# State-space mixer: chunk ends by full-width table loads, whole state tiles, and a reordered gated unit

## The chip, the cores and the metric

The kernel runs on 1 core of one Trainium2 chip. The metric is device time in microseconds (us) of one execution. A profile of one execution of the kernel before is at hand, and three timed runs of it.

## The reference, cut to what matters

Six layers run over 256 positions of 1024 channels. Each of the first four is a mixer and a gated feed-forward layer; the second of these has the state-space mixer (S5), and only that mixer is touched here. It works in 64 groups of 16 channels, each with 64 complex states, once forward and once backward over the sequence:

```python
u = hf.reshape(b, s, S5_GROUPS, S5_GROUP)            # 64 groups of 16 channels
y_fwd = _s5_direction(u, ..., False)                 # h[t] = lam_bar * h[t-1] + B_bar u[t];  y[t] = Re(C h[t])
y_bwd = _s5_direction(u, ..., True)
y = (y_fwd + y_bwd).reshape(b, s, d) + d_skip * hf
g = gelu(y)
val, gate = split(g @ w_glu, 2, axis=-1)             # the gated unit
return val * sigmoid(gate)
```

## The kernel before, in words

All matrices that are not small are multiplied as three products of split weights (`whi`, `wlo`) and split activations; a slab of weights of 128x1024 is loaded by SP's queue, split by ACT (L170) and DVE (L171), and gives 12 products of 512 columns (L307 to L309). Everything is issued in the order in which the Python code runs; a small scheduler `S` only delays pieces of code by a number of ticks, and a slab gives two ticks.

The mixer (`S5.mix`) cuts the 256 positions into 32 chunks of 8. `U` holds the input so that a column is one chunk of one group: for group (m, q) the tile `u_of(m, q)` is 128 rows (8 positions of 16 channels) by 32 chunks. Tables made earlier turn this into chunk states and back:

- **Chunk ends** (`chunk_ends`, L1703 to L1715; `place`, L1717 to L1727). For each of eight k, eight matmuls with the 32 columns of `u_of` stationary and 256 table columns (`wb`) moving, four of them side by side in column tiles of 32. The result has chunks on its partitions, so ACT copies it to `ends` (L1715), PE transposes it in four pieces (L840), and DVE and ACT put the two directions (partitions 0 to 63 forward, 64 to 127 backward) into `es` (L1724, L1726, L1727). `es[0]` takes k = 0 to 3, `es[1]` takes k = 4 to 7.
- **The scan** (`scan_ops`, L1750). For each `es`, 30 steps over the chunks of three DVE operations each (L1757, L1758, L1761), so 90 operations. The first `ISC` = 45 operations of `es[0]`'s scan run alone; after that each of them is followed by one of `es[1]`'s. What is left of `es[1]`'s scan runs alone.
- **States copied** (`states`, L1766). At chunks 11, 23 and 30 the steps done are copied by ACT from `es` to `H` (L1771, L1772), four copies for each stretch: real and imaginary parts lie in two tiles `H`, each for both scans.
- **Outputs of the mixer** (`part`, L1776). Within a chunk: `u_of` stationary and a table `local` moving, for all k, while the scan runs. From the state at the chunk's start: `H` stationary and a table `ct` moving, for k = 0 to 3 after the first scan, for k = 4 to 7 after the second. The sums are in four PSUM banks `ybank`; DVE transposes a bank (L1850), ACT does the gelu (L1846), and ACT and DVE split it (L453, L454).
- **The gated unit** (`in_proj`). Sixteen slabs (b, s): output block b of 512 columns, input channels 256s to 256s+255. Slabs with s of 0 or 1 need the outputs of k = 0 to 3 alone, those with s of 2 or 3 also those of k = 4 to 7. Four slabs with s of 0 or 1 come first. The function `rest` (the products for k = 4 to 7 and their outputs) is put into the order of PE after `OR` = 6 ticks, so behind 36 products.

The tables for k = 3 to 7, `local` and `ct` come from DRAM by SP's queue; tiles of 128x2048 share 13 buffers. `taps` (L1573) makes `local` in the feed-forward layer before the mixer, by small matmuls (L1579).

Of the kernel before, what the change touches and what calls it, by code (L numbers as in the profile page):

```python
# [17 lines left out]
P = 128  # L18
# [17 lines left out]
BB = 12  # L36
AR = 13
GD = 3
ISC = 45


DS = (0, 1, 2, 3, 4, 4, 5, 5)
# [5 lines left out]
IK = 3  # L48
OB = 0
OS = 2  # L50
OR = 6
QD = 7
AE = 4
ISM = 1000
# [154 lines left out]
def tile_two_blocks(ctx: ExitStack, tc: tile.TileContext, A, out, upto=None, taps=None):  # L209
# [37 lines left out]
            o += [(b, s) for s in range(4)]  # L247
        return o

    def add_in(ap, nblk, base=0):  # L250
        for b, s in order_in(nblk):
            W.add(ap[base + b, s])

    def add_out(ap, nk, order=None):
# [4 lines left out]
    for i in (range(6) if upto is None else upto):  # L259
        if i >= 4:  # L260
            i -= 4
            layers.append(("ffn1", i))
            add_in(A["ffn1_in"][i], 11)
            add_out(A["ffn1_out"][i], 22)
            layers.append(("mix", i))
            for b, s in order_in(12)[:8]:
                W.add(A["mix_in"][i, b, s])
            W.add(A["mix_small"][i])
            for b, s in order_in(12)[8:]:
                W.add(A["mix_in"][i, b, s])  # L270
            add_out(A["mix_out"][i], 16)
            layers.append(("ffn2", i))
            add_in(A["ffn2_in"][i], 11)
            add_out(A["ffn2_out"][i], 22)
            continue
        kind = i % 3
        if kind == 0:
            layers.append(("fourier", i))
            W.add(A["dft_d"])
            W.add(A["dft_t"])  # L280
            add_out(A["fnet_w_out"][i // 3], 8)
        elif kind == 2:
            layers.append(("attention", i))
            add_in(A["qkv"], 18)
            add_out(A["attn_o"], 8, ATTN_OUT)
        else:
            layers.append(("s5", i))
            add_in(A["s5_glu"], 4)
        layers.append(("ffn", i))
        add_in(A["ffn_in"][i], 11)  # L290
        add_out(A["ffn_out"][i], 22)
# [119 lines left out]
            if i % 2 == 1:  # L411
                S.tick()

    def in_proj(xn, nblk, evict, src=None, after_head=None, bank=lambda b: acc()):

        head = {}
        for b, s in order_in(nblk):
# [883 lines left out]
    class S5:  # L1301
# [267 lines left out]
        def taps(self, m, ct):  # L1569
# [102 lines left out]
        def mix(self, xn, nxt):  # L1672
# [28 lines left out]
                return U[:, q * 512 + m * 32:q * 512 + (m + 1) * 32]  # L1701

            es = [big(F32, "es") for _ in range(2)]  # L1703
            ends = {}
# [12 lines left out]
            def place(k):  # L1717

                e = ends.pop(k)
                ps = transposed([e[:, u * 256 + r * P:u * 256 + (r + 1) * P] for r in range(2) for u in range(2)])  # L1720
                src = ps.rearrange("p (r g c) -> p r g c", r=2, g=8)
                dst = es[k // 4].rearrange("p (c r g) -> p r g c", r=2, g=32)[:, :, k % 4 * 8:k % 4 * 8 + 8]
                if k < 4:
                    nc.vector.tensor_copy(dst[:64], src[:64])  # L1724
                else:
                    nc.scalar.activation(dst[:64], src[:64], AF.Copy)  # L1726
                nc.scalar.activation(dst[64:], src[64:, :, :, ::-1], AF.Copy)  # L1727
# [16 lines left out]
            H = [big(F32, "H") for _ in range(2)]  # L1744
            for r in range(2):
                h = H[r].rearrange("p (g c) -> p g c", g=64)
                nc.gpsimd.memset(h[:64, :, 0:1], 0.0)
                nc.gpsimd.memset(h[64:, :, 31:32], 0.0)

            def scan_ops(w):  # L1750

# [4 lines left out]
                for c in range(1, 31):  # L1756
                    yield lambda: nc.vector.tensor_tensor(t, a8, e[:, c - 1, None].to_broadcast([P, 2, 2, 32]), OP.mult)  # L1757
                    yield lambda: nc.vector.tensor_tensor(e[:, c], e[:, c], t[:, 0], OP.add)  # L1758

                    def last():  # L1760
                        nc.vector.tensor_tensor(e[:, c], e[:, c], swapped, OP.add)  # L1761
                        if c in (11, 23, 30):
                            states(w, c - 11 if c < 30 else 24, c + 1)
                    yield last

            def states(w, c0, c1):  # L1766
                src = es[w].rearrange("p (c r g) -> p r g c", r=2, g=32)
                gs = slice(32 * w, 32 * w + 32)
                for r in range(2):
                    h = H[r].rearrange("p (g c) -> p g c", g=64)  # L1770
                    nc.scalar.activation(h[:64, gs, c0 + 1:c1 + 1], src[:64, r, :, c0:c1], AF.Copy)  # L1771
                    nc.scalar.activation(h[64:, gs, 31 - c1:31 - c0], src[64:, r, :, c0:c1][:, :, ::-1], AF.Copy)  # L1772

            ybank = [acc() for _ in range(4)]

            def part(k, i, local=None):  # L1776
                for s in range(2):
                    m = 2 * k + s
                    for q in range(4):
                        o = ybank[k // 2][32 * q:32 * q + 32, k % 2 * 256:(k % 2 + 1) * 256].rearrange(  # L1780
                            "p (j s k) -> p j s k", j=8, s=2)[:, :, s]
                        g = 4 * m + q
                        if i == 0:
                            lhs, rhs = u_of(m, q), local[:, m % 4 * 512 + q * P:m % 4 * 512 + (q + 1) * P]
                        else:
                            lhs = H[i - 1][:, g * 32:(g + 1) * 32]
                            at = s * 1024 + q * 256 + (i - 1) * P
                            rhs = self.ct[k][:, at:at + P]
                        nc.tensor.matmul(o, lhs, rhs, start=i == 0 and s == 0 and k % 2 == 0, stop=i == 2,
                                         skip_group_check=True, tile_position=(0, 32 * q))  # L1790

            local = [self.load_local(i) for i in range(4)]
            for k in range(4):
                self.load_ct(k)
            for k in range(8):
                part(k, 0, local[k // 2])
            for k in range(4, 8):
                self.load_ct(k, local[k - 4])
            first, second = scan_ops(0), scan_ops(1)
# [3 lines left out]
                    next(second)()  # L1803
            oT = Chunks(8)
            for k in range(4):
                for i in (1, 2):
                    part(k, i)
# [7 lines left out]

            def rest():
                for k in range(4, 8):
                    for i in (1, 2):
                        part(k, i)
# [256 lines left out]
```

## Time and profile before

| | us |
|---|---|
| median of 3 runs | 2505.49 (2505.14 to 2505.72) |
| the profiled execution | 2506.46 |
| its span in the trace | 2504.7 |
| PE busy | 2437.3 (97%) |
| DVE busy | 1620.1 (65%) |
| ACT busy | 1330.6 (53%) |

A row of the trace gives the time from the start of the span, the time taken, the engine and the line. PE is TensorE's matmuls, PEld its loads of the stationary operand. "x16" is a number of records; a float32 matmul leaves two records, each with a load and a product. Granted clock is that of TensorE, as a share of full speed: 1.00 is 2.4 GHz and 0.50 is 1.2 GHz. The chain of work that ended last is followed back from the end: each piece in it was released by the one before it.

### The profile page before, as it was taken

The page shows a single profiled execution, that of the slowest core. Times are in us where ns is not written, and L with a number is a line of the kernel's source. Part 1 is how long each engine was busy: PE and PEld are TensorE (multiplying, and loading weights), DVE is VectorE, ACT ScalarE, POOL GpSimd, SP SyncE. Part 2 cuts the span into 40 slices and gives each one's busy share as a digit, 9 for nine tenths or more (in the row PEclk, how much of TensorE's full clock was granted, in tenths as well). Part 3 has the DMA queues.
Part 4 walks back from the last instruction along what each step waited for, and adds up shares of the span by engine and source line. Part 5 has one row for each costly group of instructions (what it writes and reads, how often), then busy time and mean ns, then how long its engine had stood idle before and what let it go on. Part 6 is the DMA issues. An engine that isn't in the chain of part 4 may idle for free.

```text
span 2504.7 us, 34769 instructions
## 1 busy us (share of the span) xinstructions
PE 2437.3 (97%) x13048; PEld 2008.2 (80%) x13048; DVE 1620.1 (65%) x2855; ACT 1330.6 (53%) x2029; POOL 101.7 (4%) x123
## 2 busy tenths in 40 slices
PE   7999869999999999999999999999999999999998
PEld 6777658888878788888888888888888888788886
DVE  7989866555776665565555557875555555876554
ACT  5444565444565554444444446765444445775543
POOL 0011000000043200000000000000000000000000
PEclk9999979999999999999999999999999999999999
DMA  5798655565555455535555554545556565535554
GB/s 173 235 285 250 239 206 187 183 200 189 164 164 175 146 185 184 188 125 190 191 180 190 192 181 153 178 135 188 181 185 195 176 188 176 193 121 168 185 185 143
DMA packets 132424, 460.53 MB, mean 184 GB/s; under 512 B 14857, under 2 KB 23956, under 8 KB 129312
## 3 DMA queue, kind: packets, MB, share of 16 engines
q1 hardware_dynamic: 124192, 431.16, 53.3%
q0 software_dynamic: 7488, 26.51, 3.3%
q8 instruction: 102, 1.67, 0.3%
q10 hardware_dynamic: 576, 0.66, 0.1%
q14 instruction: 66, 0.54, 0.1%
HBM read 441.76 MB, written 20.69 MB: 185 GB/s over the span
## 4 chain that ended last, share of the span: by engine, by line
PE 88%; DVE 7%; ACT 4%; issue 1%; DMA 0%; POOL 0%; ACTq 0%; DVEq 0%; POOLq 0%
PE acc L307 26%; PE acc L308 26%; PE acc L309 26%; DVE wlo L171 2%; PE aux L473 2%; PE aux L840 1%; DVE conv L1002 1%; ACT whi L170 1%; PE aux L381 1%; PE aux L745 1%; PE aux L696 1%; PE aux L722 1%; PE aux L1579 0%; PE aux L1238 0%; PE aux L659 0%
## 5 line engine op out<-in xcount | busy, mean ns | idle before, releaser
L171 DVE TENSOR_TENSOR wlo<-raw,whi 128x1024 fp32r<-128x1024 f32 (+1 forms) x774 | 924.6, 1218 | 386.9 <-ACT whi L170 380.7
L170 ACT ACTIVATE whi<-raw 128x1024 fp32r<-128x1024 f32 (+1 forms) x774 | 794.2, 1056 | 319.7 <-PE acc L309 294.6
L307 PE MATMUL acc<-whi,xhi 128*128 128x512 f32 (+1 forms) x2104 | 836.6, 398 | 2.4 <-DVE yflo L519 2.4
L308 PE MATMUL acc<-wlo,xhi 128*128 128x512 f32 (+1 forms) x2104 | 819.9, 390 | 7.4 <-DVE wlo L171 7.4
L309 PE MATMUL acc<-whi,xlo 128*128 128x512 f32 (+1 forms) x2104 | 819.7, 390 | 0.0
L308 PEld LDWEIGHTS acc<-wlo,xhi 128*128 128x128 f32 x2104 | 396.8, 189 | 85.8 <-DVE wlo L171 9.8
L307 PEld LDWEIGHTS acc<-whi,xhi 128*128 128x128 f32 x2104 | 396.8, 189 | 84.8 <-issue 4.4
L309 PEld LDWEIGHTS acc<-whi,xlo 128*128 128x128 f32 x2104 | 396.2, 188 | 82.7
L307 PE MATMUL acc<-whi,yhi 128*128 128x512 f32 x976 | 386.2, 396 | 2.4 <-ACT whi L170 0.9
L308 PE MATMUL acc<-wlo,yhi 128*128 128x512 f32 x976 | 380.8, 390 | 3.2 <-DVE wlo L171 3.2
L309 PE MATMUL acc<-whi,ylo 128*128 128x512 f32 x976 | 381.0, 390 | 0.0
L484 ACT ACTIVATE silu<-acc,rsq 128x256 f32<-128x256 f32 x176 | 83.6, 475 | 304.2 <-PE acc L309 304.2
L485 DVE SCALAR_TENSOR_TENSOR hb<-acc,rsq,silu 128x256 f32<-128x256 f32 x176 | 84.5, 483 | 222.6 <-ACT silu L484 222.5
L308 PEld LDWEIGHTS acc<-wlo,yhi 128*128 128x128 f32 x976 | 183.4, 188 | 41.2 <-DVE wlo L171 4.8
L307 PEld LDWEIGHTS acc<-whi,yhi 128*128 128x128 f32 x976 | 183.3, 188 | 41.0 <-ACT whi L170 1.3
L309 PEld LDWEIGHTS acc<-whi,ylo 128*128 128x128 f32 x976 | 183.2, 188 | 39.6 <-DVE ylo L454 0.9
L453 ACT ACTIVATE yhi<-aux 128x512 fp32r<-128x512 f32 (+1 forms) x104 | 54.3, 562 | 105.2 <-PE aux L473 102.7
L454 DVE TENSOR_TENSOR ylo<-aux,yhi 128x512 fp32r<-128x512 f32 (+1 forms) x104 | 63.7, 644 | 56.6 <-ACT yhi L453 56.5
L390 ACT ACTIVATE xhi<-aux,gains 128x256 fp32r<-128x256 f32 x104 | 40.7, 475 | 82.2 <-PE aux L381 82.2
L392 DVE SCALAR_TENSOR_TENSOR xlo<-aux,gains,xhi 128x256 fp32r<-128x256 f32 x104 | 43.1, 477 | 49.9 <-ACT xhi L390 49.9
L436 DVE SCALAR_TENSOR_TENSOR x<-acc,x 128x512 f32<-128x512 f32 x52 | 35.5, 690 | 55.9 <-PE acc L309 55.9
L715 POOL TENSOR_SCALAR sc<-sc,st 128x512 f32<-128x512 f32 x28 | 46.7, 1673 | 268.7 <-DVE st L713 256.9
(361 smaller groups left out, 1794.1 us busy)
## 6 DMA issues: line engine op xcount, KB each, us to landing
raw<-in_ffn_in_dram SPq DMA_DIRECT2D x352, 512.0 KB, 4.3
raw<-in_ffn_out_dram SPq DMA_DIRECT2D x176, 512.0 KB, 4.3
raw<-in_mix_in_dram SPq DMA_DIRECT2D x96, 512.0 KB, 3.6
raw<-in_qkv_dram SPq DMA_DIRECT2D x72, 512.0 KB, 4.1
raw<-in_mix_out_dram SPq DMA_DIRECT2D x32, 512.0 KB, 3.7
raw<-in_fnet_w_out_dram SPq DMA_DIRECT2D x16, 512.0 KB, 4.3
s_ct<-s5set POOLq DMA_DIRECT2D x16, 512.0 KB, 5.1
raw<-in_s_glu_dram SPq DMA_DIRECT2D x16, 512.0 KB, 4.5
```

The source lines that it names most:

```text
L170: self.nc.scalar.activation(hi[:, :w], r, AF.Copy)
L171: self.nc.vector.tensor_tensor(lo[:, :w], r, hi[:, :w].bitcast(F32), OP.subtract)
L307: nc.tensor.matmul(ps, lhs.hi, rhs.hi, start=start, stop=False, skip_group_check=True)
L308: nc.tensor.matmul(ps, lhs.hi, rhs.lo, start=False, stop=False, skip_group_check=True)
L309: nc.tensor.matmul(ps, lhs.lo, rhs.hi, start=False, stop=stop, skip_group_check=True)
L392: nc.vector.scalar_tensor_tensor(lo, p, g, hi.bitcast(F32), OP.mult, OP.subtract)
L453: nc.scalar.activation(p.hi, ps, AF.Copy)
L454: nc.vector.tensor_tensor(p.lo, ps, p.hi.bitcast(F32), OP.subtract)
L473: nc.tensor.transpose(pt[:, u * T + t * P:u * T + (t + 1) * P], hb[:, t * 256 + u * P:t * 256 + (u + 1) * P], ident)
L484: nc.scalar.activation(s, ps[t][:, :256], AF.Silu, scale=r)
L485: nc.vector.scalar_tensor_tensor(hb[:, t * 256:(t + 1) * 256], ps[t][:, 256:], r, s, OP.mult, OP.mult)
L715: (nc.vector if u == 3 and e else nc.gpsimd).tensor_scalar(s, s, st[:, 3:4], None, OP.mult)
```

## The change

Six edits, all in the S5 mixer's code but for the order of its gated unit's weights:

1. `chunk_ends` makes the table stationary (128 columns) and `u_of` moving (32 columns): 16 matmuls for each k over the whole array. The result has states on its partitions, so there is no copy to `ends` and no transpose; `place` reads it from PSUM. The order is now chunk ends and `place` of k = 0, 1, then the second half of the input (`f[3]`, `gather`), then k = 2 to 7.
2. `es` is shifted by one chunk with a zero first chunk (written by POOL, which before zeroed the edges of `H`), so that it holds the state that enters each chunk. The scan has 30 steps as before, and pairs the two scans from operation `ISC` = 30.
3. `states` copies at four chunks, real and imaginary parts in one copy, and each scan has an `H` tile of its own. The last stretch has four chunks, and its forward half is copied by DVE.
4. `part` is split into `within` and `entering`; `entering(k)` does all real parts of k and then all imaginary parts.
5. The gated unit takes six slabs with s of 0 or 1 first (`GLU_IN`; its weights are loaded and split in that order too), and `rest` comes after `OR` = 5 ticks, so behind 30 products. Block 2 uses `aux` banks.
6. In `taps`, the matmuls for q = 3 have 32 stationary columns in place of 16, for all m but the last.

```diff
-ISC = 45
+ISC = 30
-OR = 6
+OR = 5
+GLU_IN = tuple((b, s) for h in range(2) for b in range(3) for s in (2 * h, 2 * h + 1)) \
+    + tuple((3, s) for s in range(4))
...
-                n = 16 if q == 3 else 32
+                n = 16 if g == 63 else 32
...
             def chunk_ends(k):
-                ps = aux()
+                ends[k] = ps = aux()
                 for u in range(2):
-                    for q in range(4):
-                        m = 2 * k + u
-                        nc.tensor.matmul(ps[32 * q:32 * q + 32, u * 256:(u + 1) * 256], u_of(m, q),
-                                         self.wb[k][:, u * 1024 + q * 256:u * 1024 + (q + 1) * 256],
-                                         start=u == 0, stop=True, skip_group_check=True, tile_position=(0, 32 * q))
-                ends[k] = tmp(name="ends")
-                nc.scalar.activation(ends[k], ps, AF.Copy)
+                    for r in range(2):
+                        for q in range(4):
+                            at, o = u * 1024 + q * 256 + r * P, (r * 8 + u * 4 + q) * 32
+                            nc.tensor.matmul(ps[:, o:o + 32], self.wb[k][:, at:at + P], u_of(2 * k + u, q),
+                                             start=True, stop=True)
 
             def place(k):
-                e = ends.pop(k)
-                ps = transposed([e[:, u * 256 + r * P:u * 256 + (r + 1) * P] for r in range(2) for u in range(2)])
-                src = ps.rearrange("p (r g c) -> p r g c", r=2, g=8)
+                src = ends.pop(k).rearrange("p (r g c) -> p r g c", r=2, g=8)
...
             for k in range(2):
                 chunk_ends(k)
-            for k in range(2, 4):
-                place(k - 2)
-                chunk_ends(k)
-            for k in range(2, 4):
                 place(k)
             for f in second:
                 f[3]()
             self.gather(1)
-            for k in range(4, 8):
+            for k in range(2, 8):
                 chunk_ends(k)
-                if k >= 5:
-                    place(k - 1)
-            place(7)
+                place(k)
...
-                        if c in (11, 23, 30):
-                            states(w, c - 11 if c < 30 else 24, c + 1)
+                        if c in (10, 20, 27, 31):
+                            states(w, {10: 0, 20: 11, 27: 21, 31: 28}[c], c + 1)
...
+                if c1 == 32:
+                    nc.vector.tensor_copy(dst[:64, :, :, c0:c1], src[:64])
+                else:
+                    nc.scalar.activation(dst[:64, :, :, c0:c1], src[:64], AF.Copy)
+                nc.scalar.activation(dst[64:, :, :, 32 - c1:32 - c0], src[64:, :, :, ::-1], AF.Copy)
...
-            in_proj(xn, 4, evict, src=lambda b: oT, bank=lambda b: (aux if b == 1 else acc)())
+            in_proj(xn, 4, evict, src=lambda b: oT, bank=lambda b: (aux if b in (1, 2) else acc)(),
+                    order=GLU_IN)
```

On PE, from the first chunk ends to the first products with states, the order before was (L1711 chunk ends, L840 transposes, L1656 the second half of the input, L1789 the mixer's outputs):

```order
L1711 MATMUL aux<-s5wb,U 32x256 x8
L1711 MATMUL aux<-wb,U 32x256 x8
L840 MATMUL aux<-ident,ends 128x128 x4
L1711 MATMUL aux<-wb,U 32x256 x8
L840 MATMUL aux<-ident,ends 128x128 x4
L1711 MATMUL aux<-wb,U 32x256 x8
L840 MATMUL aux<-ident,ends 128x128 x8
L1656 MATMUL acc<-ident,hq 128x32 x32
L1711 MATMUL aux<-wb,U 32x256 x16
```

and it is now (L1717 chunk ends, L1658 the second half of the input, L1780 and L1792 the outputs, L309 the gated unit):

```order
L1717 MATMUL aux<-U,s5wb 128x32 x16
L1717 MATMUL aux<-U,wb 128x32 x16
L1658 MATMUL acc<-ident,hq 128x32 x32
L1717 MATMUL aux<-U,wb 128x32 x96
L1780 MATMUL acc<-local,U 32x8x16 x64
L1792 MATMUL acc<-ct,H 32x8x16 x64
L309 MATMUL acc<-whi,yhi 128x512
```

The 64 narrow matmuls with 32 transposes have become 128 full-width ones, and the second half of the input stands behind two of the eight k in place of four.

On ACT, at the end of the paired scans, the order before was (es_3126 and es_3127 are the first and the second scan's tiles, H_3312 and H_3313 real and imaginary states):

```order
L1771 ACTIVATE H_3313<-es_3127 64x32x12
L1772 ACTIVATE H_3313<-es_3127 64x32x12
L1771 ACTIVATE H_3312<-es_3126 64x32x7
L1772 ACTIVATE H_3312<-es_3126 64x32x7
L1771 ACTIVATE H_3313<-es_3126 64x32x7
L1772 ACTIVATE H_3313<-es_3126 64x32x7
L1846 ACT_TABLE_LOAD
```

and it is now (H_3438 and H_3501 are the states of the first and the second scan):

```order
L1765 ACTIVATE H_3438<-es_3126 64x64x7
L1766 ACTIVATE H_3438<-es_3126 64x64x7
L1765 ACTIVATE H_3501<-es_3127 64x64x10
L1766 ACTIVATE H_3501<-es_3127 64x64x10
L1766 ACTIVATE H_3438<-es_3126 64x64x4
L1849 ACT_TABLE_LOAD
```

The first scan's last stretch is one ACT copy in place of four, and two copies of the second scan's states stand directly ahead of it.

## Rows read from the trace of the kernel before

**Rows 1.** The page, part 2: granted clock, 40 slices.
```profile
PEclk9999979999999999999999999999999999999999
```

**Rows 2.** Stretches: busy us of PE, PEld, DVE, ACT, POOL; granted clock; DMA share, GB/s.
```profile
296.00:299.00 3.00, 3.00 (x26) 1.86 (x27) 3.00 (x8) 0.18 (x1) 0.00 (x0) 0.51 0.96 404
300.00:306.00 6.00, 4.65 (x61) 2.67 (x60) 3.51 (x5) 4.64 (x6) 0.00 (x0) 1.00 0.88 274
327.00:343.00 16.00, 4.45 (x80) 4.06 (x84) 10.61 (x65) 10.55 (x13) 0.00 (x0) 0.50 0.81 336
358.00:364.00 6.00, 3.67 (x68) 2.99 (x72) 2.07 (x5) 3.39 (x5) 0.00 (x0) 0.50 0.01 3
```

**Rows 3.** Chain of work that ended last, 289 to 370: start, us, what.
```profile
295.89 4.17 PE aux L1711 x32
...
321.62 1.09 ACT es L1727
322.73 0.29 DVE s5t L1757
...
329.23 0.40 DVE s5t L1757 x2
...
330.18 0.40 DVE s5t L1757 x2
...
339.63 2.83 PE acc L1789 x48
342.48 0.73 DVE y L1850
...
353.07 0.30 DVE s5t L1757
...
353.91 0.30 DVE s5t L1757
...
358.72 0.24 DVE es L1761
...
361.41 4.67 PE acc L1789 x112
366.08 0.43 PE aux L307
```

**Rows 4.** Timeline of PEld, full-width float32 loads: start, us, engine, line, operation, count.
```profile
294.64 0.30 PEld L1685 LDWEIGHTS acc<-s5pick,s5sel 128*128 128x128 f32 x2 [2.78 <-DVE s5pick L1683]
...
1545.87 0.74 PEld L1073 LDWEIGHTS aux<-dt,tri 128*128 128x128 f32 x6 [0.31 <-issue]
...
1585.99 0.30 PEld L1143 LDWEIGHTS aux<-xnat,seg 128*128 128x128 f32 x2 [0.54 <-ACT seg L1132]
1586.21 0.30 PEld L1144 LDWEIGHTS aux<-xnat,seg 128*128 128x128 f32 x2
```

**Rows 5.** Timeline of PE, 300 to 355.
```profile
300.58 1.07 PE L1711 MATMUL aux<-wb,U 128*32 128x256 f32 x16
...
305.84 0.75 PE L1656 MATMUL acc<-ident,hq 32*128 32x32 f32 x32
...
352.63 0.39 PE L307 MATMUL aux<-whi,yhi 128*128 128x512 f32 x1
...
354.45 0.39 PE L309 MATMUL aux<-whi,ylo 128*128 128x512 f32 x1
```

**Rows 6.** Groups by line and shape, 290 to 402: count, busy us, mean ns, idle before.
```profile
L1727 ACT ACTIVATE es<-aux 64x512 f32<-64x512 f32 x8 | 8.6, 1073 | 1.9 <-DVE es L1724 1.7
L1771 ACT ACTIVATE H<-es 64x384 f32<-64x384 f32 x8 | 7.0, 878 | 8.1 <-DVE es L1761 8.1
L1771 ACT ACTIVATE H<-es 64x224 f32<-64x224 f32 x4 | 2.3, 587 | 2.4 <-DVE es L1761 2.3
```

**Rows 7.** Stretches of 1 us, PE alone: busy us, records, granted clock, DMA share, GB/s.
```profile
362.00:363.00 1.00, 1.00 (x28) 0.50 0.00 0
...
365.00:366.00 1.00, 1.00 (x40) 1.00 0.71 217
```

**Rows 8.** Line L1579 (taps): records, least, median and greatest ns, first and last start.
```profile
L1579 PEld LDWEIGHTS aux<-s5set,s5bb x512: 89/106/107, 82.1 to 181.3; 64*32 64x32 f32 x129, 64*16 64x16 f32 x42
```

More of the change, by code (lines that the diff above doesn't have):

```diff
@@ L248, in order_in, with add_in @@
         return o
-    def add_in(ap, nblk, base=0):
-        for b, s in order_in(nblk):
+    def add_in(ap, nblk, base=0, order=None):
+        for b, s in order or order_in(nblk):
             W.add(ap[base + b, s])
@@ L287, in tile_two_blocks @@
             layers.append(("s5", i))
-            add_in(A["s5_glu"], 4)
+            add_in(A["s5_glu"], 4, order=GLU_IN)
         layers.append(("ffn", i))
@@ L412, in slab_step, with in_proj @@
                 S.tick()
-    def in_proj(xn, nblk, evict, src=None, after_head=None, bank=lambda b: acc()):
+    def in_proj(xn, nblk, evict, src=None, after_head=None, bank=lambda b: acc(), order=None):
         head = {}
-        for b, s in order_in(nblk):
+        for b, s in order or order_in(nblk):
             if b not in head:
@@ L1703, in mix @@
             es = [big(F32, "es") for _ in range(2)]
+            for e in es:
+                nc.gpsimd.memset(e[:, :64], 0.0)
             ends = {}
             def chunk_ends(k):
-                ps = aux()
+                ends[k] = ps = aux()
                 for u in range(2):
-                    for q in range(4):
-                        m = 2 * k + u
-                        nc.tensor.matmul(ps[32 * q:32 * q + 32, u * 256:(u + 1) * 256], u_of(m, q),
-                                         self.wb[k][:, u * 1024 + q * 256:u * 1024 + (q + 1) * 256],
-                                         start=u == 0, stop=True, skip_group_check=True, tile_position=(0, 32 * q))
@@ L1720, in place @@
[L1720 to L1722 removed]
+                src = ends.pop(k).rearrange("p (r g c) -> p r g c", r=2, g=8)
+                dst = es[k // 4].rearrange("p (c r g) -> p r g c", r=2, g=32)[:, :, k % 4 * 8:k % 4 * 8 + 8, 1:]
                 if k < 4:
[L1724 removed]
+                    nc.vector.tensor_copy(dst[:64], src[:64, :, :, :31])
@@ L1725, in place @@
                 else:
-                    nc.scalar.activation(dst[:64], src[:64], AF.Copy)
-                nc.scalar.activation(dst[64:], src[64:, :, :, ::-1], AF.Copy)
+                    nc.scalar.activation(dst[:64], src[:64, :, :, :31], AF.Copy)
+                nc.scalar.activation(dst[64:], src[64:, :, :, :0:-1], AF.Copy)
             for k in range(2):
                 chunk_ends(k)
-            for k in range(2, 4):
-                place(k - 2)
-                chunk_ends(k)
-            for k in range(2, 4):
@@ L1738, in mix @@
             self.gather(1)
-            for k in range(4, 8):
+            for k in range(2, 8):
                 chunk_ends(k)
-                if k >= 5:
-                    place(k - 1)
-            place(7)
[L1744 to L1748, printed above, removed]
+                place(k)
             def scan_ops(w):
@@ L1755, in scan_ops @@
                 e = es[w].rearrange("p (c r g) -> p c r g", r=2, g=32)
-                for c in range(1, 31):
+                for c in range(2, 32):
                     yield lambda: nc.vector.tensor_tensor(t, a8, e[:, c - 1, None].to_broadcast([P, 2, 2, 32]), OP.mult)
@@ L1761, in last, with outputs_of, within @@
                         nc.vector.tensor_tensor(e[:, c], e[:, c], swapped, OP.add)
-                        if c in (11, 23, 30):
-                            states(w, c - 11 if c < 30 else 24, c + 1)
+                        if c in (10, 20, 27, 31):
+                            states(w, {10: 0, 20: 11, 27: 21, 31: 28}[c], c + 1)
                     yield last
             def states(w, c0, c1):
[L1767 to L1772, printed above, removed]
+                if w not in H:
+                    H[w] = big(F32, "H")
+                src = es[w].rearrange("p (c r g) -> p r g c", r=2, g=32)[:, :, :, c0:c1]
+                dst = H[w].rearrange("p (r g c) -> p r g c", r=2, g=32)
+                if c1 == 32:
[3 more added lines that the diff above has]
+                nc.scalar.activation(dst[64:, :, :, 32 - c1:32 - c0], src[64:, :, :, ::-1], AF.Copy)
+            H = {}
             ybank = [acc() for _ in range(4)]
-            def part(k, i, local=None):
+            def outputs_of(k, s, q):
+                return ybank[k // 2][32 * q:32 * q + 32, k % 2 * 256:(k % 2 + 1) * 256].rearrange(
+                    "p (j s k) -> p j s k", j=8, s=2)[:, :, s]
+            def within(k, local):
                 for s in range(2):
@@ L1779, in part, with entering @@
                     for q in range(4):
[L1780 to L1789, printed above, removed]
-                                         skip_group_check=True, tile_position=(0, 32 * q))
+                        nc.tensor.matmul(outputs_of(k, s, q), u_of(m, q),
+                                         local[:, m % 4 * 512 + q * P:m % 4 * 512 + (q + 1) * P],
+                                         start=s == 0 and k % 2 == 0, stop=False,
+                                         skip_group_check=True, tile_position=(0, 32 * q))
+            def entering(k):
+                h = H[k // 4].rearrange("p (r g c) -> p r g c", r=2, g=32)
+                for r in range(2):
+                    for s in range(2):
+                        for q in range(4):
+                            at = s * 1024 + q * 256 + r * P
+                            nc.tensor.matmul(outputs_of(k, s, q), h[:, r, k % 4 * 8 + 4 * s + q],
+                                             self.ct[k][:, at:at + P], start=False, stop=r == 1,
+                                             skip_group_check=True, tile_position=(0, 32 * q))
             local = [self.load_local(i) for i in range(4)]
@@ L1795, in mix @@
             for k in range(8):
-                part(k, 0, local[k // 2])
+                within(k, local[k // 2])
             for k in range(4, 8):
@@ L1805, in mix @@
             for k in range(4):
-                for i in (1, 2):
-                    part(k, i)
+                entering(k)
             between = iter([f for b in range(2) for f in self.outputs(b, ybank[b], oT)])
@@ L1817, in rest @@
                 for k in range(4, 8):
-                    for i in (1, 2):
-                        part(k, i)
+                    entering(k)
                 fs = [self.outputs(b, ybank[b], oT) for b in (2, 3)]
```

## The prediction

> **What bounds the kernel now.** I read the page first, for where the kernel is not simply PE at work. The granted clock is at full level in every slice but one [rows 1], and that slice and the end of the one before are the S5 mixer; everything else is a stream of 512-column products that the change leaves alone, but for small matmuls in `taps`. Then the stretches: PE is at its lower level, 1.2 GHz, from 296 to 299, through 327 to 343, where it has 4.45 us of work in 16, and from 358 to 364 [rows 2]. Then the chain, which gives what the mixer waits for [rows 3]. Chunk ends start at 295.89. The last `place` by ACT starts at 321.62, and at 322.73 DVE starts the paired scans. They run to about 337, the states are copied, PE runs the products from them at 339.63, DVE transposes the first bank at 342.48, and the second scan ends at 358.96 (358.72 + 0.24). PE takes its states up at 361.41 and is back in the gated unit at 366.08. From there on PE has no idle time, so what reaches that point later, reaches the end later.
>
> So I carry five dates through: start of paired scans (322.73), first transpose (342.48), end of the second scan (358.96), return to the gated unit (366.08), and the products still to do there.
>
> **The change, part by part.**
>
> *Chunk ends.* Before, eight narrow matmuls for one k leave 16 records in 1.07 us at 2.4 GHz [rows 5], and ACT, PE and DVE pass the result on between them. Now each k has 16 full-width float32 matmuls, so 32 loads of 128 columns, with only 32 columns to stream. No row has this in bulk. The nearest are four small places with loads of just this width: two take 0.30 us and six take 0.74 us, so four more cost 0.44, 0.11 each; and two pairs stand 0.22 apart, again 0.11 each [rows 4]. The products behind them have 16, 32 and 64 columns, and the spacing is the same, so the load sets it. I take 0.11 us, for 256 of them. From below I bound it by 0.067 us (1.07/16 [rows 5]), what a narrow record costs, from above by 0.215 us, the same 0.11 at the lower clock: the first 32 narrow records took 4.17 us [rows 3] at 0.51 [rows 2], 0.130 each against 0.067, a factor of 1.95.
>
> PE has been idle when it starts, and before the clock was low until about 299.5. I let it do the same: 3.6 us at 0.215 gives 16 or 17 loads, and 240 at 0.11 give 26.4. With 0.75 for the second half of the input [rows 5] PE ends at 295.9 + 3.6 + 26.4 + 0.75 = 326.6. ACT's two copies for a k take 2.1 us [rows 6], less than PE's 3.5, so they hide under PE but for the last pair: `es[1]` is complete at about 328.8 instead of 322.7, **6.1 us later**. `es[0]` is complete near 313.7, so 31 operations of the first scan (8.8 us at the single-step rate below) are done by 322.5, and DVE then waits 6 us. The copies to `ends`, the transposes and one hand-over for each k are gone, but they were cheaper than the loads that replace them.
>
> A rule speaks to this edit. The Trainium skill, "TensorEngine Tiling (Array Packing)", sections "Theoretical Speedup" and "When to Use Tiling", says that an operand of 32 columns should be made stationary and packed four ways, for up to four times the speed: this is the form that the change gives up. Held to its four times, the 128 narrow records (8.6 us) would become 34.2 us in place of my 28.2 at full clock, and the sum would be 6 us longer. The rows come nearer, since they time the load itself.
>
> *Pairing.* With `ISC` 30 the paired steps are 20 instead of 15, and 10 steps of the second scan are left instead of 15. A paired step takes 0.95 us (330.18 - 329.23), a single one 0.84 (353.91 - 353.07) [rows 3]. So the first transpose moves by **+4.75**, and the end of the second scan gains **4.2** back.
>
> *States.* A copy of 384 elements takes 0.88 us and one of 224 takes 0.59 [rows 6], 1.8 ns an element over 0.17. By that 704 elements take 1.45, 640 take 1.33, 448 take 0.98 and 256 take 0.64. At the end of the paired scans ACT has two copies of the second scan (2.66 us) to do, released one paired step earlier, and then the last of the first (0.64): 2.5 us from the scan's end to PE, with a hand-over. Before it was 2.65 (322.73 and 15 steps of 0.95 give 336.98; PE ran from 339.63). That is **-0.2**. But before, a first batch of 16 records ran ahead of that, and only 48 were needed (2.83 us); now it is all 64: **+1.0**. After the second scan DVE and ACT copy the last four chunks side by side, 0.64 us and a hand-over, where PE waited 2.45 (361.41 - 358.96): **-1.7**.
>
> *The outputs from states.* The 128 records for k = 4 to 7 take 36 ns each at the lower clock and 25 at the higher [rows 7]. Before, PE had been idle over 5 us and the last 112 took 4.67 [rows 3]. Now PE has 30 products ready behind the first transpose (36 took until 354.8 [rows 5]), so it waits about 2.4 us, and I take 4.2 for all 128, between 3.3 and 4.7: **-0.4**.
>
> *The gated unit.* Six products fewer lie ahead of `rest`, so six more follow it. Eight products are 1.82 us apart [rows 5], 0.228 each: **+1.4**. Behind `rest` now stand 42 products that need none of its outputs, 9.6 us; before there were 12, 2.7 us, and they were enough. Weight splits of the next slabs stand behind the outputs on ACT and DVE, but have those 9.6 us. Nothing is gained, since nothing was waited for.
>
> *Small things, 0.* In `taps` a narrow load grows from about 89 ns to 107 [rows 8], 18 ns on a quarter of the loads, four tiles side by side: for 180 loads under 1 us, more likely nothing, and below nothing only if equal shapes pack better. POOL zeroes two tiles instead of four strips, long ahead. SP's queue keeps its order: two `local` tables come earlier, and `ct` waits for later chunk ends, but has 20 us and more until it is needed. The new `H` tiles wait for chunk ends of k = 6 and 7, which are over before ACT gets to them.
>
> **The sum.** First transpose: 6.1 + 4.75 - 0.2 + 1.0 = 11.65 later. End of the second scan: 11.65 - 4.2 = 7.4. Back in the gated unit: 7.4 - 1.7 - 0.4 = 5.3. With the six products: 6.7, which I round to **+6.5 us**. The profiled execution took 2506.46, so the changed one 2513.0; it lies 0.97 above the median of the runs, 2505.49, so the forecast is **2512.0**. Its own range, with loads between 0.105 and 0.118 us, 1.5 us each for the first clock and for the copies, is 2508 to 2517.
>
> **The rivals.**
>
> *The clock stays low through the chunk ends (slower still).* PE would be occupied without a gap for some 30 us, but mostly with loads: 32 columns are streamed for every 128 loaded. For it: no row shows the clock rising in such a stretch; where it rose after a start at 0.51, narrow products of 256 columns ran without a gap [rows 2, 5]. Against it: PE has no idle time there. The price is 256 x 0.215 = 55.0 instead of 30.0, and 0.7 for the rest of the stretch: 25.7 more, **2537.7**. It decides if the clock is below 1.00 after 303. The Trainium skill, "TensorE: Matmul & The Clock Gate", Part 1, says that the clock is set by how busy PE has recently been; it does not say whether loads count.
>
> *The tiling rule's four times holds (slower still).* Then the loads cost 0.134 us, the place is the same, and the time is 6 us above the forecast: **2518**.
>
> *The load hides, and ACT sets the pace (not slower).* If consecutive full-width loads overlapped in bulk, a record could cost 0.067 us. Then PE needs 2.1 us for a k, like ACT's two copies; `es[1]` would be ready at about 317.6, 11.2 us ahead of my date, and the time would be **2500.8**. It decides below 0.087 us a load, where the sum is zero. Against it stand all the rows 4: with 16 columns to stream the spacing was still 0.11. For it speaks only that the rows show two, four and six such loads, not 256 of them.
>
> That the change does not do what it says can be left out: the order shows all six edits.
>
> **How the numbers follow.** Forecast 0.50, low clock 0.28, tiling rule 0.08, hidden load 0.10, anything else 0.04. The range goes from 2503, below the forecast's own range, to 2539, above the low clock's time; the hidden load is left out. About 0.2% (5 us) is what a measurement of this kernel can tell from no change. Slower by more: two thirds of the forecast, the low clock and the tiling rule, 0.70. Within: a third of the forecast (0.17) and half of the hidden load (0.05), 0.22. Faster: 0.08.
>
> **What would show it.** Right: loads of the chunk ends 0.11 us apart, clock 1.00 from about 300, PE without a gap until 326 to 327, DVE idle some 6 us ahead of the paired scans, which start near 329; first transpose near 354; PE back in the gated unit near 371. The states step is wrong if PE waits over 3 us after the first scan's end, the pairing step if a paired step is not 0.95. The forecast is wrong if paired scans start before 323, or if the clock reads 0.50 in the chunk ends after 303.

## The result, and the profile after

The changed kernel takes 2538.12 us (median of 4 runs, 2537.33 to 2539.9) against 2505.6 for the kernel before in the same comparison: a ratio of 1.0132, with a 95% interval from 1.012 to 1.0144, so about 32.5 us slower. The number that was predicted, 2512.0, is 26 us too low; the rival of the low clock gave 2537.7. The profiled execution took 2538.40, and the differences below are between this one and the 2506.46 of before.

The page of the changed kernel: part 1 in its first line, then the granted clock in 40 slices, as in [rows 1].

```profile
PE 2473.5 (98%) x13144; PEld 2053.9 (81%) x13144; DVE 1618.4 (64%) x2857; ACT 1324.3 (52%) x2011; POOL 101.2 (4%) x121
...
PEclk9999859999999999999999999999999999999999
```

PE is busy for 36 us more (2473.5 against 2437.3), and in the fifth and sixth slice, 254 to 380 us, the clock reads 8 and 5 where it read 9 and 7. So PE does not wait longer, it works more slowly, and the stretches say where (columns as in [rows 2]):

```profile
296.00:312.00 16.00, 15.83 (x101) 15.73 (x102) 7.56 (x15) 1.93 (x2) 0.00 (x0) 0.50 0.88 345
312.00:332.00 20.00, 20.00 (x95) 20.00 (x95) 6.93 (x23) 2.44 (x4) 0.00 (x0) 0.50 0.66 250
332.00:352.00 20.00, 20.00 (x95) 19.96 (x94) 3.19 (x13) 5.71 (x6) 0.00 (x0) 0.50 0.29 106
```

From 312 to 352 PE is busy without any gap, its loads too, and the granted clock is 0.50, that is 1.2 GHz, throughout. In the kernel before, the chunk ends also started low (0.51), but were at 1.00 from 300 on [rows 2]. The transfers are no reason that shows: the clock stays the same while the DMA share goes from 0.88 to 0.29.

The timeline of PE shows the records of the chunk ends (L1717; L1658 is the second half of the input between them, L1780 the outputs within a chunk):

```profile
296.17 7.01 PE L1717 MATMUL aux<-U,s5wb 128*128 128x32 f32 x32 [0.83 <-DVE U L1693]
302.99 7.01 PE L1717 MATMUL aux<-U,wb 128*128 128x32 f32 x32
309.94 1.07 PE L1658 MATMUL acc<-ident,hq 32*128 32x32 f32 x32
310.93 41.17 PE L1717 MATMUL aux<-U,wb 128*128 128x32 f32 x192
352.03 5.66 PE L1780 MATMUL acc<-local,U 128*32 128x128 f32 x128
```

From 310.93 to 352.03 there are 192 records, 0.214 us each: the price that the prediction gave for the low clock (0.215), and not the 0.11 that it took. The chain of waits, in its columns of [rows 3], gives the dates:

```profile
296.17 13.83 PE aux L1717 x64
310.00 1.00 PE acc L1658 x23
311.00 41.11 PE aux L1717 x192
...
353.21 1.07 ACT es L1728
354.30 0.29 DVE s5t L1747
...
372.19 1.33 ACT H L1765
373.53 1.82 ACT H L1766 x2
375.39 3.69 PE acc L1792 x64
379.10 0.73 DVE y L1853
...
391.46 0.64 ACT H L1766
392.14 3.70 PE acc L1792 x128
395.84 0.43 PE aux L309
```

One step of the chunk ends' PE time is 41 us of this chain, where before PE, ACT and DVE passed short pieces to one another. Set beside the dates that the prediction carried through (the fourth column adds its 25.7 for the low clock to all of them):

| | before [rows 3] | forecast | with the low clock | after |
|---|---|---|---|---|
| paired scans start | 322.73 | 328.8 | 354.5 | 354.30 |
| first transpose | 342.48 | 354.1 | 379.8 | 379.10 |
| second scan ends | 358.96 | 366.4 | 392.1 | 391.4 |
| back in the gated unit | 366.08 | 371.4 | 397.1 | 395.84 |

### The profile page after: what moved, and what is told of

Its sections match the earlier page's. It is cut to its first block, busy times and chain, and to the rows that moved or that the text cites. A ratio compares the mean times of both kernels' runs of the same rounds, so it can differ in the third digit from the quotient of the medians.

```text
span 2536.6 us, 34937 instructions
## 1 busy us (share of the span) xinstructions
PE 2473.5 (98%) x13144; PEld 2053.9 (81%) x13144; DVE 1618.4 (64%) x2857; ACT 1324.3 (52%) x2011; POOL 101.2 (4%) x121
## 4 chain that ended last, share of the span: by engine, by line
PE 83%; issue 7%; DVE 6%; ACT 3%; DMA 0%; POOL 0%; ACTq 0%; DVEq 0%; POOLq 0%
PE acc L309 24%; PE acc L310 24%; PE acc L311 24%; PE aux L1717 2%; DVE wlo L173 2%; PE aux L475 1%; PE aux L842 1%; DVE conv L1004 1%; ACT whi L172 1%; PE aux L383 1%; PE aux L747 1%; PE aux L724 1%; PE aux L698 1%; PE aux L1581 0%; PE aux L1240 0%
## 5 line engine op out<-in xcount | busy, mean ns | idle before, releaser
L309 PE MATMUL acc<-whi,xhi 128*128 128x512 f32 (+1 forms) x2104 | 836.8, 398 | 2.4 <-DVE yflo L521 2.1
L309 PEld LDWEIGHTS acc<-whi,xhi 128*128 128x128 f32 x2104 | 397.1, 189 | 84.4 <-issue 4.3
L309 PE MATMUL acc<-whi,yhi 128*128 128x512 f32 x960 | 380.6, 396 | 2.7 <-ACT whi L172 0.9
L310 PE MATMUL acc<-wlo,yhi 128*128 128x512 f32 x960 | 374.9, 391 | 3.2 <-DVE wlo L173 3.2
L311 PE MATMUL acc<-whi,ylo 128*128 128x512 f32 x960 | 375.3, 391 | 0.1
L309 PEld LDWEIGHTS acc<-whi,yhi 128*128 128x128 f32 x960 | 180.7, 188 | 40.8 <-ACT whi L172 1.3
L438 DVE SCALAR_TENSOR_TENSOR x<-acc,x 128x512 f32<-128x512 f32 x52 | 35.5, 690 | 55.9 <-PE acc L311 55.9
```

The lines of the kernel that those rows point to most:

```text
L309: nc.tensor.matmul(ps, lhs.hi, rhs.hi, start=start, stop=False, skip_group_check=True)
L310: nc.tensor.matmul(ps, lhs.hi, rhs.lo, start=False, stop=False, skip_group_check=True)
L311: nc.tensor.matmul(ps, lhs.lo, rhs.hi, start=False, stop=stop, skip_group_check=True)
```

## The experiments

Two questions were open: whether edit 1 alone makes the loss, and why the clock does not rise in its stretch (the loads, or the idle time of PE ahead of it). After that, what the other edits are worth. Three kernels ran once (`e2_full_alone`, `e3_wide4`, `e4_ahead`); they are read by differences of 4 us and more, the others by repeated runs.

### Edit 1 undone, and edit 1 alone

`e1_tiled` is the changed kernel with the old `chunk_ends`, its transposes in `place`, and the old order of both:

```diff
-                            nc.tensor.matmul(ps[:, o:o + 32], self.wb[k][:, at:at + P], u_of(2 * k + u, q),
-                                             start=True, stop=True)
+                        nc.tensor.matmul(ps[32 * q:32 * q + 32, u * 256:(u + 1) * 256], u_of(m, q),
+                                         self.wb[k][:, u * 1024 + q * 256:u * 1024 + (q + 1) * 256],
+                                         start=u == 0, stop=True, skip_group_check=True, tile_position=(0, 32 * q))
...
+                ps = transposed([e[:, u * 256 + r * P:u * 256 + (r + 1) * P] for r in range(2) for u in range(2)])
```

> The changed kernel with edit 1 undone (narrow matmuls, copy to ends, transposes; the other five edits stay). Theory A, the sum of the prediction with the low clock in the chunk ends: all of the loss is edit 1, and the other five edits are worth 4.75 - 0.2 + 1.0 - 4.2 - 1.7 - 0.4 + 1.4 = +0.65 us, so 2506.3, between 2504 and 2508; es[1] complete at 322.7, first transpose near 348.0, second scan end near 360.3. Rival B, the other edits carry part of the loss (copies of the second scan ahead of the first's, six slabs, the new pairing): 2510 or more.

Measured: 2505.14 us (11 runs), ratio to before 0.9996, interval 0.9987 to 1.0005. The five other edits together move nothing that can be measured, and theory A's +0.65 is inside the interval.

`e2_full_alone` is the reverse, the kernel before with the new `chunk_ends`, `place` from PSUM and the new order:

```diff
-                                         self.wb[k][:, u * 1024 + q * 256:u * 1024 + (q + 1) * 256],
+                            nc.tensor.matmul(ps[:, o:o + 32], self.wb[k][:, at:at + P], u_of(2 * k + u, q),
...
-                ps = transposed([e[:, u * 256 + r * P:u * 256 + (r + 1) * P] for r in range(2) for u in range(2)])
-                src = ps.rearrange("p (r g c) -> p r g c", r=2, g=8)
+                src = ends.pop(k).rearrange("p (r g c) -> p r g c", r=2, g=8)
```

> The kernel before with edit 1 alone (full-width table loads, and the order of chunk ends and place that goes with it). Theory A: es[1] is complete at 354.3, as in the changed kernel, in place of 322.7, and everything behind it is 31.6 us later: 2537.2, between 2535 and 2539. Rival B: the other edits carry 5 us or more of the loss: 2532 or less.

Measured: 2537.97 us. Its timeline of PE has the same stretch as the changed kernel, to the hundredth:

```profile
294.99 7.01 PE L1713 MATMUL aux<-U,s5wb 128*128 128x32 f32 x32 [0.83 <-DVE U L1691]
301.81 7.01 PE L1713 MATMUL aux<-U,wb 128*128 128x32 f32 x32
308.75 1.07 PE L1656 MATMUL acc<-ident,hq 32*128 32x32 f32 x32
309.75 41.17 PE L1713 MATMUL aux<-U,wb 128*128 128x32 f32 x192
```

Edit 1 alone makes the whole loss (one run, 32.8 us above the 2505.21 of before beside it), and taking it out takes the whole loss away.

### Why the clock stays low

`e3_wide4` lets each loaded table meet 128 columns in place of 32: the same 32 columns four times. The matmuls go in rising order of `o`, so that each writes over the surplus of the one before; the loads are the same 256.

```diff
-                for u in range(2):
-                    for r in range(2):
+                for r in range(2):
+                    for u in range(2):
...
-                            nc.tensor.matmul(ps[:, o:o + 32], self.wb[k][:, at:at + P], u_of(2 * k + u, q),
+                            n = min(4, 16 - r * 8 - u * 4 - q)
+                            nc.tensor.matmul(ps[:, o:o + 32 * n].rearrange("p (n c) -> p n c", c=32),
+                                             self.wb[k][:, at:at + P],
+                                             u_of(2 * k + u, q)[:, None, :].to_broadcast([P, n, 32]),
```

> The changed kernel, each table load followed by 128 streamed columns in place of 32 (the same 32 columns four times; the surplus is overwritten by the matmuls behind it). Theory A, the clock is low because the stretch is nearly all loads: granted clock 1.00 a few us after the start, loads 0.11 us apart, chunk ends 30 to 34 us in place of 55, the time 2513 to 2518. Rival C, the clock is low because PE stood idle ahead of 296 and stays at the level that it starts with: 0.50 to the end, loads 0.215 apart or more, 2538 or more.

`e4_ahead` leaves the loads as they are and fills PE's idle time ahead of them, with five matmuls of 512 columns (ten records) around the one for `s5rows`:

```diff
             ps = acc()
+            for i in range(3):
+                nc.tensor.matmul(ps, ident, self.wb[0][:, 512 * i:512 * i + 512], start=True, stop=True)
             nc.tensor.matmul(ps[:, :32], self.sel[:, :P], pick, start=True, stop=True)
+            ps2 = acc()
+            for i in range(2):
+                nc.tensor.matmul(ps2, ident, self.wb[0][:, 512 * i:512 * i + 512], start=True, stop=True)
```

> The changed kernel with five 512-column products put into PE's idle time between 292 and 297, whose results nobody reads, so that the chunk ends start at a granted clock of 1.00; the loads are as they were. Theory A: the clock falls to 0.50 within some us of the start and stays there until the outputs; the loads are 0.11 us apart at first, then 0.215; 2535 to 2539. Rival C: it stays at 1.00, all loads 0.11 apart, 28 us for the chunk ends in place of 55: 2510 to 2514.

Measured: 2514.21 us for `e3_wide4`, 2533.51 for `e4_ahead`. The timeline of PE in `e3_wide4`, and its stretches (columns as in [rows 2]):

```profile
294.46 5.75 PE L1718 MATMUL aux<-U,s5wb 128*128 128x128 f32 x32 [0.84 <-DVE U L1693]
300.05 3.74 PE L1718 MATMUL aux<-U,wb 128*128 128x128 f32 x32
303.72 0.69 PE L1658 MATMUL acc<-ident,hq 32*128 32x32 f32 x32
304.34 21.62 PE L1718 MATMUL aux<-U,wb 128*128 128x128 f32 x192
325.89 3.70 PE L1783 MATMUL acc<-local,U 128*32 128x128 f32 x128
```

```profile
296.00:300.00 4.00, 4.00 (x27) 4.00 (x25) 2.90 (x5) 0.00 (x0) 0.00 (x0) 0.66 0.50 156
300.00:303.00 3.00, 3.00 (x29) 3.00 (x28) 1.00 (x1) 1.02 (x1) 0.00 (x0) 1.00 0.90 283
...
312.00:318.00 6.00, 6.00 (x56) 6.00 (x56) 4.44 (x16) 3.08 (x3) 0.00 (x0) 1.00 1.01 415
```

With four times the columns the same 192 records take half the time, 21.55 us or 0.112 each, because the clock is at 1.00 from 300 on. And `e4_ahead`:

```profile
295.36 3.65 PE L1722 MATMUL aux<-U,s5wb 128*128 128x32 f32 x32
298.85 6.01 PE L1722 MATMUL aux<-U,wb 128*128 128x32 f32 x32
304.79 1.07 PE L1658 MATMUL acc<-ident,hq 32*128 32x32 f32 x32
305.79 41.17 PE L1722 MATMUL aux<-U,wb 128*128 128x32 f32 x192
```

```profile
295.40:299.00 3.60, 3.60 (x35) 3.60 (x33) 3.59 (x7) 0.00 (x0) 0.00 (x0) 1.00 0.64 214
299.60:303.00 3.40, 3.40 (x20) 3.40 (x19) 0.46 (x1) 1.00 (x1) 0.00 (x0) 0.55 0.97 319
303.00:304.70 1.70, 1.70 (x9) 1.70 (x9) 0.00 (x0) 0.00 (x0) 0.00 (x0) 0.50 0.96 361
```

Here PE had no idle time ahead, and the first 32 loads, at 1.00, are 0.109 apart. Then the clock falls to 0.50 in the midst of the chunk ends, with PE busy all along, and the last 192 records take their 41.17 again. So the idle time ahead of the stretch is not the reason. The columns behind each load, and the order of the loads within a k, are all that `e3_wide4` changed in PE's work, and with 128 columns the clock reads 1.00 where it reads 0.50 with 32. No run had a number between 32 and 128. Theory A stands in both. Its number for `e4_ahead` is a miss: 2533.51 lies below the range from 2535 to 2539. The stretch from the first chunk end to the outputs took 51.5 us in place of 55.9, so the loads at full clock were worth most of the 4.6 us.

The two together also settle the price of a load: 0.109 us with 32 columns behind it and 0.112 with 128, both at 1.00. The load sets the spacing.

### What the other edits are worth

With narrow chunk ends PE still waited ahead of the second scan's end. Three kernels take `e1_tiled` and change two numbers; one takes the kernel before.

```diff
 e5_pair51
-ISC = 30
+ISC = 51
-OR = 5
+OR = 8
 e6_pair45
-ISC = 30
+ISC = 45
-OR = 5
+OR = 6
 e7_pair45_or8
-ISC = 30
+ISC = 45
-OR = 5
+OR = 8
 e8_before_or8, from the kernel before
-OR = 6
+OR = 8
```

> The changed kernel with edit 1 undone, the scans paired from operation 51 and 48 products of the gated unit ahead of rest. Theory A: es[1] is complete when the first scan has done about 51 operations, so its end comes 2 paired steps earlier than with 45 (1.9 us), and in the kernel before PE had no work for 5 to 6 us ahead of the second scan's end, so 12 products more fit there: 2.7 us for the products, 2.0 to 2.8 for the copies and outputs after the second scan, and up to 0.5 for the pairing below the kernel before: 2500.0, between 2498 and 2502.5. Rival B, the weights of the further slabs are not split in time or the outputs of k = 4 to 7 come too late for the products behind rest: 2504 or more.

> The changed kernel with edit 1 undone and the two numbers of the kernel before (paired from 45, 36 products ahead of rest), so the new states, six slabs and taps stay. Theory A: the copies after the second scan and the outputs at a higher clock give 2 to 2.8 us, the products of rest are covered: 2503.0, between 2502 and 2504.5. Rival B, the new states give nothing because the end of the first scan is later: 2505 or more.

> As the one before, with 48 products ahead of rest in place of 36. Theory A: PE waits for the second scan there, so the 12 products are free: 2.7 us below it, 2500.3, between 2499 and 2502. Rival B, no gain since the products behind rest then wait for the outputs: as the one before, 2503.

> The kernel before with 48 products ahead of rest in place of 36; its first four slabs are then used up, and no product that can do without the outputs of rest is left behind it. Theory A, the six slabs are needed for this: PE waits some 3 us for the outputs, the gain of 2.7 is given back, 2505 to 2506.5. Rival B, the wait is short and the order of the slabs is worth nothing: 2502.5 to 2503.5.

| | us, 11 runs | ratio to before | interval |
|---|---|---|---|
| e5_pair51 | 2502.70 | 0.9990 | 0.9981 to 0.9998 |
| e6_pair45 | 2502.71 | 0.9991 | 0.9982 to 1.0 |
| e7_pair45_or8 | 2499.17 | 0.9977 | 0.9968 to 0.9986 |
| e8_before_or8 | 2505.28 | 1.0004 | 0.9995 to 1.0013 |

`e7_pair45_or8` beats both kernels, by 6 us against before (the interval gives 3.5 to 8), and lies in theory A's range. The number of `e6_pair45` lies in theory A's range too, but its interval reaches 1.0, and its trace does not show the reason that theory A gave: from the second scan's end to the gated unit it is 6.4 us for 7.12 before, and the products of `rest` took nearly as long as before (5.72 us for 5.89). `e8_before_or8` came as its theory A had it. In it the 12 products are paid back: the timeline of its PE has a wait of 3.34 us behind `rest` for the outputs of k = 4 to 7, since no slab of the first channels is left.

```profile
365.01 0.50 PE L307 MATMUL acc<-whi,yhi 128*128 128x512 f32 x1 [3.34 <-ACT yhi L453]
```

So `OR` = 8 without the six slabs gives nothing that can be measured. The six slabs without `OR` = 8 did not run by themselves: `e6_pair45` has the new states and the new `taps` besides.

`e5_pair51` is a miss: 2500.0 was expected, 2502.70 lies just above the range, and it is 3.5 us behind `e7_pair45_or8`. The timelines of PE, first product of the gated unit and products of `rest`, of `e5_pair51`:

```profile
341.43 0.50 PE L309 MATMUL acc<-whi,yhi 128*128 128x512 f32 x1 [0.78 <-ACT yhi L455]
...
357.76 6.16 PE L1801 MATMUL acc<-local,H 128*32 128x128 f32 x128 [3.77 <-ACT H L1775]
```

and of `e7_pair45_or8`:

```profile
342.99 0.50 PE L309 MATMUL acc<-whi,yhi 128*128 128x512 f32 x1 [0.95 <-ACT yhi L455]
...
357.64 3.70 PE L1801 MATMUL acc<-local,H 128*32 128x128 f32 x128 [2.09 <-ACT H L1775]
```

and their stretches from 356 to 362, of `e5_pair51`:

```profile
356.00:362.00 6.00, 4.24 (x80) 3.93 (x84) 4.21 (x8) 2.63 (x3) 0.00 (x0) 0.50 0.08 23
```

and of `e7_pair45_or8`:

```profile
356.00:362.00 6.00, 4.36 (x131) 4.07 (x132) 4.49 (x9) 2.91 (x4) 0.00 (x0) 1.00 0.17 41
```

The earlier end of the first scan only brings the gated unit forward (341.43 against 342.99); the second scan does not end sooner. So PE is through with its 48 products earlier, waits 3.77 us instead of 2.09, and takes the products of `rest` at 0.50 in 6.16 us instead of 3.70 at 1.00. Those 2.46 us are about what the two profiled executions differ by (2501.17 and 2498.97); the medians differ by 3.5.

Why the second scan does not end sooner can be read beside `e6_pair45`. The last copy into `es[1]`, the start of the paired scans and the products of `rest`, first of `e5_pair51` (the last row stands above):

```profile
317.87 1.08 ACT L1731 ACTIVATE es<-aux 64x496 f32<-64x496 f32 x1
...
321.20 0.49 DVE L1756 TENSOR_TENSOR s5t<-s5a,es 128x128 f32<-128x128 f32 x2
```

and then of `e6_pair45`:

```profile
317.84 1.09 ACT L1731 ACTIVATE es<-aux 64x496 f32<-64x496 f32 x1
...
319.45 0.49 DVE L1756 TENSOR_TENSOR s5t<-s5a,es 128x128 f32<-128x128 f32 x2
...
355.26 5.72 PE L1801 MATMUL acc<-local,H 128*32 128x128 f32 x128 [4.79 <-ACT H L1775]
```

`es[1]` is complete at 318.95 and 318.93, but with 51 the second scan waits until 321.20 for the first one to get that far, and its states reach PE 2.5 us later (357.76 against 355.26). The premise of theory A, that `es[1]` is complete when the first scan has done about 51 operations, did not hold in this execution: in it and in `e6_pair45` the 32 records of k = 4 and 5 took 2.91 us, in `e7_pair45_or8` and in the kernel before 4.61, with the same code for them.

That a long wait is what lowers the clock was not tried by itself, and the length of the wait alone does not settle it. The same 12 products were worth 3.5 us between `e6_pair45` and `e7_pair45_or8`, not 2.7, and there too the longer wait (4.79) goes with slower products (5.72). But two kernels with full-width loads and 128 columns waited no longer than `e7_pair45_or8`, and their clock fell to 0.50 all the same, in `e3_wide4` only after the products had begun at 0.99. `e3_wide4`, then `e9_wide4_45_8` of the next section:

```profile
366.08 5.37 PE L1795 MATMUL acc<-local,H 128*32 128x128 f32 x128 [1.95 <-ACT H L1769]
```

```profile
365.50 5.37 PE L1795 MATMUL acc<-local,H 128*32 128x128 f32 x128 [2.06 <-ACT H L1769]
```

### Edit 1 at its best

`e9_wide4_45_8` is `e3_wide4` with the numbers of `e7_pair45_or8`:

```diff
-ISC = 30
+ISC = 45
-OR = 5
+OR = 8
```

> The changed kernel with 128 streamed columns behind each table load, as e3_wide4, and the two numbers of e7_pair45_or8 (paired from 45, 48 products ahead of rest). Theory A: the two numbers are worth what they were worth with narrow chunk ends (from 2505.1 to 2499.2, 6.0 us), so 2514.2 - 6.0 = 2508.2, between 2506 and 2510, and edit 1 costs 9 us against e7_pair45_or8 even where the clock is high and the rest is tuned to it. Rival B: with a later es[1] the first scan has more of its operations behind it, so that the narrow form's lead shrinks to 5 us or less: 2504 or less.

Measured: 2506.06 us (10 runs, 2504.7 to 2512.78) beside 2506.18 for before; ratio 1.0002, interval 0.9992 to 1.0011. It lies at the lower edge of theory A's range, and the 9 us for edit 1 came out smaller. Against the ratio of `e7_pair45_or8`, 0.9977, it is 0.25%, or 6 us, for the full-width form, with a high clock in its loads and the two numbers tuned (the two intervals together leave about 3 to 9.5 us). Where these 6 us lie the trace does not tell, since the profiled execution took 2509.78, 3.7 above the median: in it `es[1]` is complete 7.6 us later after the start of the chunk ends than in the profile of `e7_pair45_or8` (34.1 against 26.5), and `rest` has the 1.67 us of the low clock shown above. The low clock in the chunk ends adds some 24 us (2538.1 against 2514.2, the latter a single run).

## Why the prediction was right or wrong

The direction and the range held; the number did not. The range held because it was drawn up to the rival with the low clock: the forecast's own range, 2508 to 2517, did not. **The step that failed** is in "Chunk ends", where PE starts at the low clock and "I let it do the same", that is rise after 3.6 us as before. It never rose: 3.6 + 26.4 us became 6.82 + 6.95 + 41.10 [rows 2 against the stretches above]. The case was there as a rival, with its price (25.7 us; the start of the paired scans came 25.5 later than the forecast's 328.8) and its test ("if the clock reads 0.50 in the chunk ends after 303"), and the time it gave, 2537.7, is 0.4 off. It got 0.28 where the forecast got 0.50. The argument against it was that "PE has no idle time there", and it was worth nothing: `e4_ahead` and the changed kernel both show PE busy without a gap while the clock is low or falls.

The Trainium skill, "TensorE: Matmul & The Clock Gate", Part 1, which says that the clock follows how busy PE has been of late, is not borne out if busy is read as the profile counts it: PE has 20.00 us of work in 20.00 at 0.50, and its loads fill the 20.00 too.

The rest of the sum, each term from the dates in the table:

- **Price of a load, 0.11 us: right.** 0.109 and 0.112 at full clock, from bounds of 0.067 and 0.215; the low clock gave 0.214. `e3_wide4`, with the high clock, tests the rest of the forecast's sum: its chunk ends started at 294.46, 1.43 us earlier than before, and with this added its paired scans start at 329.6 where the forecast had 328.8, its first transpose at 354.4 for 354.1, and it is back in the gated unit at 372.9 for 371.4. It takes 2514.21 where the forecast had 2512.0.
- **Pairing and first scan: nearly right.** From the start of the paired scans to the first transpose it is 24.80 us against 19.75 before, +5.05, where 4.75 - 0.2 + 1.0 = 5.55 was summed. The 64 records took 3.69 of it, where 2.83 + 1.0 was said.
- **Second scan: right.** From the first transpose to its end 12.3 against 16.48, -4.1 for -4.2.
- **States and outputs behind it: under-sized.** From the second scan's end to the gated unit it is 4.4 against 7.12, -2.7 where -1.7 - 0.4 was summed. The wait of PE is 0.7, as said; the 128 records, close behind PE's 30 products, took 3.70 at 1.00 instead of 4.2.
- **The gated unit: right.** From its resumption to the second group of transposes for the next layer the kernel takes 1.2 us longer, for the six products (1.4). This is read at the second row of L381 before and of L383 after, in the chains:

```profile
406.82 0.87 PE aux L381 x8
```

```profile
437.80 0.87 PE aux L383 x8
```

  They are 30.98 apart, and the returns to the gated unit 29.76. Another 0.96 us lies in the 2100 us behind, where its place is not known.
- **Small things: right.** Chunk ends start at 296.17 against 295.89, so `taps` cost nothing that shows. With the new `taps` that start lies anywhere from 294.46 to 297.11 in the profiles, with the old from 294.78 to 295.89, so a cost under 1 us would not be seen.

The sum is 31.6 + 5.05 - 4.1 - 2.7 + 1.2 + 0.96 = 32.0, beside 2538.40 - 2506.46 = 31.94. It closes by the way it is made, from differences of dates and a remainder of 0.96; what it tells is the size of each term.

**The other rivals.** The tiling rule's four times: at full clock 256 loads of 0.112 make 28.7 us for the 8.6 of the narrow form [rows 5], 3.3 times. So the Trainium skill, "TensorEngine Tiling (Array Packing)", "Theoretical Speedup", has the right direction here and nearly the size. As they were found, the full-width form all at the low clock and the narrow one in part, it is 54.9 us for the 13.2 of the narrow records before (4.17, 1.07, 1.07, 4.61, 1.18 and 1.07), 4.2 times. The load that hides is excluded, since 0.112 in bulk is what the small places of [rows 4] gave.

## What to carry to other kernels

Price a long stretch of loads with a few columns streamed behind each at the low clock, here 0.21 us for 128 float32 columns with 32 behind them, until a profile shows it high; in this kernel a full busy row of PE went with either level. Make the narrow operand stationary, or stream more columns per load, even repeated ones: where the load sets the spacing, they cost next to nothing (0.109 against 0.112 us) and here gave back 24 us. And where PE waits for a scan, work put into the wait saves its own time. It may save the clock of what follows too: behind waits of 3.8 us and more the products of `rest` were at 0.50 here, behind waits of about 2 us at 1.00 in four kernels (such as the changed one and `e7_pair45_or8`) and at 0.50 in two, so look at the granted clock before counting on it.

## What the runs showed of the hardware

- PE was busy without a gap at 1.2 GHz for 55 us, and in `e4_ahead` its clock fell from 1.00 to 0.50 in the midst of unbroken work. I had expected a fall only behind idle time.
- The same code can meet another clock from one execution to the next: the 32 narrow records of k = 4 and 5 took 2.91 us at 1.00 in the profile of `e5_pair51` and 4.61 at 0.50 in that of `e7_pair45_or8`.
- Streaming the same columns four times made the same loads twice as fast (0.214 to 0.112 us each).
